# The border between two trunk layers: squares summed in two groups of eight, and the first weight splits of layer 1 in an order fixed by hand

## The chip, the cores and the metric

The kernel runs on one core of a Trainium2 chip. A core has five engines that run side by side and meet through semaphores: TensorE (PE in the profile, with its weight loads as PEld), VectorE (DVE), ScalarE (ACT), GpSimd (POOL) and SyncE (SP, which here only issues DMAs). Each engine works through its own instructions in order. The metric is the device time of one execution in microseconds (us), as the median of several runs. In this kernel a difference of about 0.2% can be told from no change.

## The reference, cut to what matters

Two layers work on 256 latent tokens and 256 context tokens of width 2048. In each layer both streams are normalised, scaled and shifted, go through one wide input projection, three mixing branches and an output projection. The border is the end of layer 0 and the start of layer 1 for the latents:

```
for l in range(DEPTH):
    ...
    h = rmsnorm(x, g_pre[l]) * (1.0 + scale[:, None]) + shift[:, None]
    proj = h @ w_in[l]
    ...
    y = rmsnorm(y @ w_out[l], g_post[l])
    x_new = x + gate[:, None] * y
```

So at the border the output projection y of layer 0 is divided by its own root mean square and added to x, which gives x1; then the root mean square of x1 over all 2048 features must be known before the first h of layer 1 exists. Everything is float32.

## The kernel before, in words

**Layout.** Activations lie transposed: `yo[k]`, k = 0 to 15, holds 128 features by 512 tokens, the latents in columns 0 to 255 (`LAT`), the context in the rest (`CTX`). `hh[k]` and `hl[k]` are the input of a projection, split into a high part (a cast to a shorter float32 form) and a low part (the difference), so that a product takes three matmuls (`mm3`, L424 to L426).

**Weights.** `Stream` brings the weights in tiles of 128 x 1024. SP loads a tile into `raw` (L382, three buffers, shared with the tiles of x that the border reads, L1118). ACT casts it to `whi` (L402), DVE subtracts to get `wlo` (L404); four buffers each. I call the first three tiles of layer 1 w0, w1 and w2. The first block of layer 1 (k = 0 and 1, `start_av` and `start_au`) needs w0 and w1, the second block w2.

**Who sets the order.** PE's instructions run in the order in which the program writes them. DVE, ACT and SP are ordered by a planner that models times and priorities; `low(n)` lowers a priority, and `tc.issue_after(x)` puts an instruction behind x on x's engine, without a semaphore. `W.behind` lists, for a weight tile by its number, what its cast must stand behind.

**The held units.** The last three output units of layer 0 (`HELD = 3`) are computed for the latents first and for the context afterwards (`hold_unit`). The context part is 48 steps of three matmuls, and covers the border's chain on PE. After each step `later.tick` adds 0.324 to a counted clock (0.648 x 256 / 512), and a task whose time has come writes its next piece into PE's order at that place. So a task's `yield` value sets after which of the 48 steps its next matmuls stand.

**The border** is the task `boundary`:

- `rms_of`: sums of y's squares (`col_sums`, L462), mean on DVE (L452), the power -1/2 on POOL (L454), spread over 128 partitions by PE (`bcast`, L475).
- For each k: DVE multiplies `yo[k]` by the factor (L1128), DVE (even k) or POOL (odd k) adds x (L1129), ACT squares it (L1132).
- PE sums the squares over the partitions with `ones`, four k side by side in four column strips (L1139). Before, this stands in four groups of four squares, after steps 15, 19, 23 and 27.
- DVE copies the sums to SBUF (`row`, L1143); PE adds the four strips (L1147, after step 30); DVE and POOL make the factor (L452, L454); PE spreads it (L475, after step 38); DVE copies it (L1152). After step 48 layer 1 begins.
- `make_h` for k = 0 and 1: DVE (L502), ACT (L506, the high part), DVE (L511, the low part).

The context part of the last three units is scaled and squared by `o_evac` (ACT L996 and L520, DVE L521) at a low priority.

Before, the casts of w0 and w1 stand behind the high part of h for k = 1 (`W.behind = {len(W.out): made, len(W.out) + 1: made}`).

Of the kernel before, what the change touches and what calls it, by code (L numbers as in the profile page):

```python
# [7 lines left out]
F32 = mybir.dt.float32  # L8
F32R = mybir.dt.float32r
BF16 = mybir.dt.bfloat16  # L10
AF = mybir.ActivationFunctionType
ALU = mybir.AluOpType

P = 128
D = 2048
KT = D // P
S = 256
T = 2 * S
EPS = 1e-6
# [47 lines left out]
def trunk_kernel(ctx: ExitStack, tc: tile.TileContext, xT, xhalf, cT, wss, wsl, wmod, win, wout0, wout1, const, vec, rows,  # L67
                 wmat, bs, sink, out):
    nc = tc.nc
    V, A, G, PE, DMA = nc.vector, nc.scalar, nc.gpsimd, nc.tensor, nc.sync  # L70
# [6 lines left out]
    def sb(shape, dt, tag, bufs=1):  # L77
        cnt[0] += 1
        return pool.tile(shape, dt, tag=tag, bufs=bufs, name=f"{tag}_{cnt[0]}")

    def w2k(shape, dt=F32):
        return sb(shape, dt, "w2k", W2K)

    def mm_ps(name="mm"):
        cnt[0] += 1
        return psum.tile([P, 512], F32, tag="mm", bufs=6, name=f"ps_{name}_{cnt[0]}")
# [6 lines left out]
    yo = [sb([P, T], F32, f"yo{k}") for k in range(KT)]  # L93
# [13 lines left out]
    class low:  # L107


        def __init__(self, n):  # L110
            self.n = n
# [8 lines left out]
    def cc(name):  # L120
        o, w = COFF[name]
        return cst[:, o - P:o - P + w]
# [151 lines left out]
    state = {"ctx": [], "phase": "", "owed": 0.0}  # L274
# [14 lines left out]
    GATES = {2: 0, 14: 1}, {7: 2}, {12: 3}, {}  # L289
    YG = 3.0  # L290
    YH = 2.0
    NX, LATE = 4, 12
    YX, YR, YC, YE = 1.0, 0.8, 1.5, 5.0
    YX1 = 12.0
    YQ, YA, YB = [5.5, 6.0], [10.0, 8.0], [3.8, 4.0]

# [45 lines left out]
    class Stream:  # L342
        AHEAD = 3

        def __init__(self):
            self.src, self.out, self.pos, self.stop = [], [], 0, 0
            self.raws = []
            self.place, self.behind = {}, {}
            for l in range(2):
                def half(name, i, h):  # L350
                    return win[l, UIDX[name][i], h]
                for i in range(2):
                    a = [half("av", 2 * i, 0), half("au01", i, 0), half("av", 2 * i, 1),
                         half("av", 2 * i + 1, 0), half("au01", i, 1), half("av", 2 * i + 1, 1)]
                    if l == 0:
                        a.insert(3 - i, half("au2", 0, i))
                        self.place[len(self.src) + 3 - i] = AU2[i]
                    self.src += a
                for i, u in enumerate(UNITS):
                    if u[0] not in ("av", "au01") + ("au2",) * (l == 0):  # L360
                        self.src += [win[l, i, 0], win[l, i, 1]]
                if l == 0:
                    self.src += [wout0[j, i] for j in range(KT) for i in range(2)]
                else:
                    self.src += [wout1[c, i] for c in range(4) for i in range(8)]
                if l == 0:
                    n = len(self.src) - 2 * HELD
                    self.place[n] = (("mraw", 2), ("mraw", 2))
                    self.place[n + 1] = (("macc", 1), ("mg", 1))
            for i, tags in enumerate(TAIL):  # L370
                self.place[len(self.src) - len(TAIL) + i] = tags
            self.raw_place = {len(self.src) - len(TAILRAW) + i: tags for i, tags in enumerate(TAILRAW)}
# [12 lines left out]
        def emitting(self, cut=1024):  # L385

            if len(self.raws) == len(self.out):
                self.load()
            n = len(self.out)
            r = self.raws[n]  # L390
            tags = self.place.get(n, (("whi", NHI), ("wlo", NLO)))
            hi, lo = ([sb([P, 1024 // len(t[0].split())], F32R, tag, t[1]) for tag in t[0].split()] for t in tags)
            self.out.append((hi, lo))
            cut = min(cut, 1024 // max(len(hi), len(lo), len(r) if isinstance(r, list) else 1))
            for i in range(0, 1024, cut):
                c = slice(i, i + cut)
                ph, pl = part((hi, lo), c)
                rc, _ = part((r, r), c)
                with ExitStack() as after:
                    for i in self.behind.get(n, ()):  # L400
                        after.enter_context(tc.issue_after(i.ins))
                    A.copy(ph, rc)  # L402
                yield
                self.last = V.tensor_tensor(out=pl, in0=rc, in1=ph.bitcast(F32), op=ALU.subtract)  # L404
                yield

        def emit(self):
# [13 lines left out]
    W = Stream()  # L421
# [6 lines left out]
    def part(w, c):  # L428

        def of(t):  # L430
            if not isinstance(t, list):
                return t[:, c]
            n = t[0].shape[-1]
            return t[c.start // n][:, c.start % n:c.start % n + c.stop - c.start]

        return of(w[0]), of(w[1])
# [12 lines left out]

    def rstd_cols(sums, n, dim):  # L450
        t = sb([P, 4], F32, "rs_a", 2)
        V.tensor_scalar(out=t[:, :n], in0=sums, scalar1=1.0 / dim, scalar2=EPS, op0=ALU.mult, op1=ALU.add)  # L452
        r = sb([P, 4], F32, "rs_b", 2)
        state["pow"] = G.tensor_tensor(out=r[:, :n], in0=t[:, :n], in1=mhalf[:, :n], op=ALU.pow)  # L454
        return r
# [67 lines left out]
    FULL, LAT, CTX = slice(0, T), slice(0, S), slice(S, T)  # L523
# [48 lines left out]
    def layer(l):  # L572
        last = l == 1
        n = S if last else T
# [16 lines left out]
        def take(k, which=(0,)):  # L591

            for i in which:
                if k % (2, 4, 8)[i] == 0:
                    ws_[i] = W.next()

        def start_av(k, ts):
            avw = ws_[0]
            c = slice((k % 2) * 512, (k % 2 + 1) * 512)
            for t in ts:  # L600
                sl = slice(t * P, (t + 1) * P)
                mm3(av[t], h_of(l, k, sl), part(avw, c), k == 0, k == KT - 1)
# [13 lines left out]
        if l == 0:  # L616
            made = {}
# [86 lines left out]
        for i, (k0, nk) in enumerate(blocks if l else ()):  # L704
            for k in range(k0, k0 + nk):
                made = make_h(1, k, rbs[0], [0])
            if i == 0:
                W.behind = {len(W.out): made, len(W.out) + 1: made}
                with tc.issue_after(made[0].ins), tc.issue_after(made[1].ins):
                    state["late"]()  # L710
            take(k0, (0, 1))
            start_av(k0, range(nt))
            if nk == 2:
                start_au(k0)
                start_av(k0 + 1, range(nt))
            start_au(k0 + nk - 1)
            if k0 == 8:
                border()
# [385 lines left out]
    def rms_of(s, acc, wait):  # L1104

        ps = ms_ps("rs")
        col_sums(ps, acc, 2)
        r = rstd_cols(ps[:, 0:2], 2, D)
        yield wait
        return bcast(r, 2)[:, 0:S]  # L1110

    def boundary(acc):

        x0s = []

        def load():
            x0s.append(sb([P, 4, S], F32, "raw", NRAW))
            DMA.dma_start(x0s[-1], xhalf[0, len(x0s) - 1])  # L1118

        for _ in range(2):  # L1120
            load()
        r0 = yield from rms_of(0, acc[:, LAT], 2.2)
        cs_ps = mm_ps("rs2")
        pend = []
        for k in range(KT):
            if k in (4, 8):
                load()
            V.tensor_tensor(out=yo[k][:, LAT], in0=yo[k][:, LAT], in1=r0, op=ALU.mult)  # L1128
            (G if k % 2 else V).tensor_tensor(out=yo[k][:, LAT], in0=yo[k][:, LAT], in1=x0s[k // 4][:, k % 4],  # L1129
                                              op=ALU.add)  # L1130
            q = w2k([P, S])
            A.activation(q, yo[k][:, LAT], AF.Square)  # L1132
            pend.append(q)
            if k % NX == NX - 1:
                yield YX
                for i, q in enumerate(pend):
                    kk = k + 1 - len(pend) + i
                    c = slice(32 * (kk % 4), 32 * (kk % 4) + 32)
                    PE.matmul(cs_ps[c, 0:S], ones[:, 0:32], q, start=kk < 4, stop=kk >= KT - 4,  # L1139
                              tile_position=(0, 32 * (kk % 4)))  # L1140
                pend = []
        row = w2k([P, S])
        V.tensor_copy(row, cs_ps[:, 0:S])  # L1143
        yield YR
        ps = ms_ps("rs")
        for j in range(2):
            PE.matmul(ps[:, j:j + 1], row[:, j * P:(j + 1) * P], cc("sel")[:, 0:1], start=True, stop=True)  # L1147
        r = rstd_cols(ps[:, 0:2], 2, D)
        yield 2.4
        rb = bcast(r, 2)  # L1150
        r = sb([P, S], F32, "rbs", 2)
        V.tensor_copy(r, rb[:, 0:S])  # L1152
        rbs[0] = r
# [46 lines left out]
    def border():  # L1200
        later.add(lowered(boundary_ctx(state["acc"])))
# [3 lines left out]
    with tc.manual_schedule(engines={EN.PE}):  # L1205
# [12 lines left out]
        for k in range(KT):  # L1218
            q = w2k([P, T])
# [7 lines left out]
        row = w2k([P, T])  # L1227
# [106 lines left out]
```

## Time and profile before

| | us |
|---|---|
| median of 3 runs (1141.18 to 1142.53) | 1141.69 |
| the profiled execution | 1141.21 |
| its span, first to last instruction | 1139.4 |
| PE busy | 1126.1 |
| DVE busy | 879.9 |
| ACT busy | 515.4 |
| POOL busy | 31.7 |

The mean granted TensorE clock is 0.998 of full speed, and DMAs move 206 GB/s on average. Between 726.5 and 746.0 us of the span, the border, PE is busy for 19.30 of 19.50 us, DVE for 12.31, ACT for 10.21 and POOL for 7.48.

In a timeline a row gives the start in us from the span's start, the duration in us, the engine, the line, the operation, the tiles (out<-in) and how many instructions are merged; in brackets stands how long the engine was idle before it and what released it. Ends of matmuls are modelled, so for PE the starts are what to read.

### The profile page before, as it was taken

The page shows a single profiled execution, that of the slowest core. Times are in us where ns is not written, and L with a number is a line of the kernel's source. Part 1 is how long each engine was busy: PE and PEld are TensorE (multiplying, and loading weights), DVE is VectorE, ACT ScalarE, POOL GpSimd, SP SyncE. Part 2 cuts the span into 40 slices and gives each one's busy share as a digit, 9 for nine tenths or more (in the row PEclk, how much of TensorE's full clock was granted, in tenths as well). Part 3 has the DMA queues.
Part 4 walks back from the last instruction along what each step waited for, and adds up shares of the span by engine and source line. Part 5 has one row for each costly group of instructions (what it writes and reads, how often), then busy time and mean ns, then how long its engine had stood idle before and what let it go on. Part 6 is the DMA issues. An engine that isn't in the chain of part 4 may idle for free.

```text
span 1139.4 us, 16858 instructions
## 1 busy us (share of the span) xinstructions
PE 1126.1 (99%) x6335; PEld 932.0 (82%) x6339; DVE 879.9 (77%) x1480; ACT 515.4 (45%) x933; POOL 31.7 (3%) x39
## 2 busy tenths in 40 slices
PE   8999999999999999999999999999999999999997
PEld 3567788888898888888888888887898988888885
DVE  1545498999987787888999993397788689868884
ACT  5222422322335667632532333365655369856551
POOL 0000000000000000000000000205000000000001
PEclk9999999999999999999999999999999999999999
DMA  9999665556655343355466664258756675555872
GB/s 353 394 390 402 243 198 194 182 185 217 201 176 175 112 139 128 106 200 184 152 220 212 215 189 143 74 177 210 221 179 211 217 274 194 170 159 194 298 260 74
DMA packets 72658, 234.28 MB, mean 206 GB/s; under 512 B 8448, under 2 KB 11392, under 8 KB 72576
## 3 DMA queue, kind: packets, MB, share of 16 engines
q1 hardware_dynamic: 70272, 231.11, 60.0%
q0 software_dynamic: 2304, 2.10, 1.2%
q8 instruction: 49, 0.80, 0.3%
q14 instruction: 33, 0.27, 0.1%
HBM read 231.08 MB, written 2.10 MB: 205 GB/s over the span
## 4 chain that ended last, share of the span: by engine, by line
PE 96%; DMA 2%; DVE 1%; ACT 0%; SPq 0%; issue 0%; POOL 0%; DVEq 0%; POOLq 0%; ACTq 0%
PE ps_t L424 14%; PE ps_t L426 14%; PE ps_t L425 14%; PE ps_t L540 10%; PE ps_t L541 5%; PE ps_y L424 3%; PE ps_y L426 3%; PE ps_y L425 3%; PE ps_mod L169 2%; PE ps_av L424 2%; PE ps_cx L426 2%; PE ps_cx L424 2%; PE ps_cx L425 2%; PE ps_av L425 2%; PE ps_av L426 2%; PE ps_tp L910 2%
## 5 line engine op out<-in xcount | busy, mean ns | idle before, releaser
L402 ACT CAST whi<-raw 128x1024 fp32r<-128x1024 f32 (+1 forms) x216 | 224.1, 1041 | 327.6 <-PE ps_t L425 193.4
L404 DVE TENSOR_TENSOR wlo<-raw,whi 128x1024 fp32r<-128x1024 f32 (+1 forms) x216 | 260.3, 1209 | 67.4 <-ACT whi L402 65.8
L424 PE MATMUL ps_t<-hh,whi 128*128 128x512 f32 (+1 forms) x704 | 268.2, 381 | 0.0
L426 PE MATMUL ps_t<-hh,wlo 128*128 128x512 f32 (+1 forms) x704 | 267.6, 380 | 0.0
L425 PE MATMUL ps_t<-hl,whi 128*128 128x512 f32 (+1 forms) x704 | 267.4, 380 | 0.0
L207 DVE SCALAR_TENSOR_TENSOR macc<-mraw,cs,macc 128x512 f32<-128x512 f32 x360 | 248.7, 744 | 15.1 <-DMA mraw<-in_wmod_dram 14.5
L540 PE MATMUL ps_t<-hh,whi 128*128 128x512 f32 x448 | 163.7, 402 | 0.0
L426 PEld LDWEIGHTS ps_t<-hh,wlo 128*128 128x128 f32 x704 | 132.4, 188 | 25.2
L424 PEld LDWEIGHTS ps_t<-hh,whi 128*128 128x128 f32 x704 | 132.4, 188 | 25.0 <-issue 1.2
L425 PEld LDWEIGHTS ps_t<-hl,whi 128*128 128x128 f32 x704 | 132.4, 188 | 23.7
L541 PE MATMUL ps_t<-hh,wlo 128*128 128x256 f32 x448 | 125.7, 281 | 0.0
L540 PEld LDWEIGHTS ps_t<-hh,whi 128*128 128x128 f32 x448 | 84.2, 188 | 19.1 <-issue 0.5
L541 PEld LDWEIGHTS ps_t<-hh,wlo 128*128 128x128 f32 x448 | 84.7, 189 | 0.5 <-issue 0.5
L506 ACT ACTIVATE hh<-w2k,sh 128x256 fp32r<-128x256 f32 x48 | 21.8, 502 | 78.5 <-DVE w2k L502 78.5
L424 PE MATMUL ps_y<-whi,hh 128*128 128x512 f32 x104 | 41.3, 397 | 0.0
L426 PE MATMUL ps_y<-whi,hh 128*128 128x512 f32 x104 | 40.6, 390 | 0.0
L425 PE MATMUL ps_y<-wlo,hh 128*128 128x512 f32 x104 | 40.5, 389 | 0.0
L424 PE MATMUL ps_av<-whi,hh 128*128 128x512 f32 x96 | 39.9, 415 | 0.6 <-ACT hh L506 0.6
L424 PE MATMUL ps_cx<-whi,hh 128*128 128x512 f32 x96 | 38.7, 403 | 0.0
L425 PE MATMUL ps_av<-wlo,hh 128*128 128x512 f32 x96 | 38.0, 396 | 0.4 <-DVE wlo L404 0.4
L425 PE MATMUL ps_cx<-wlo,hh 128*128 128x512 f32 x96 | 37.3, 389 | 0.0
L441 ACT CAST w2k<-ps_tp 128x512 fp32r<-128x512 f32 x40 | 23.4, 584 | 23.1 <-PE ps_scc L425 12.7
(398 smaller groups left out, 1860.4 us busy)
## 6 DMA issues: line engine op xcount, KB each, us to landing
raw<-in_win_dram SPq DMA_DIRECT2D x160, 512.0 KB, 4.1
mraw<-in_wmod_dram SPq DMA_DIRECT2D x128, 512.0 KB, 4.3
raw<-in_wout_dram SPq DMA_DIRECT2D x60, 512.0 KB, 4.3
mraw<-in_wsl_dram SPq DMA_DIRECT2D x16, 512.0 KB, 6.6
yo<-in_xT_dram SPq DMA_DIRECT2D x16, 256.0 KB, 5.2
macc<-in_wsl_dram SPq DMA_DIRECT2D x8, 512.0 KB, 7.6
vv<-in_wsl_dram SPq DMA_DIRECT2D x8, 512.0 KB, 8.1
mg<-in_wsl_dram SPq DMA_DIRECT2D x8, 512.0 KB, 8.0
```

What stands on the lines that cost most here:

```text
L169: PE.matmul(ps[32 * kk:32 * kk + 32, 0:n], cpad[:, kg * 4 + kk], ws[kk], start=kg == 0, stop=kg == 3, tile_position=(0, 32 * kk))
L207: V.scalar_tensor_tensor(out=acc[:, s], in0=w[:, kk % 2], scalar=c, in1=acc[:, s], op0=ALU.mult, op1=ALU.add)
L402: A.copy(ph, rc)
L404: self.last = V.tensor_tensor(out=pl, in0=rc, in1=ph.bitcast(F32), op=ALU.subtract)
L424: PE.matmul(ps, st[0], mv[0], start=start, stop=False)
L425: PE.matmul(ps, st[0], mv[1], start=False, stop=False)
L426: PE.matmul(ps, st[1], mv[0], start=False, stop=stop)
L441: A.copy(hi, src)
L506: first = A.activation(h_of(l, k, sl)[0], t[:, sl], AF.Identity, bias=sh[l][:, k, s:s + 1])
L540: PE.matmul(ps, w[0], h, start=k == 0, stop=False)
L541: PE.matmul(ps[:, 0:S], w[1], h[:, 0:S], start=False, stop=k == KT - 1)
L910: PE.transpose(tp[:, (2 * j + b) * P:(2 * j + b + 1) * P], src, ident)
```

## The change

Four things change in the code, all at the border.

1. The squares are summed in two groups of eight. ACT writes them in pairs into one buffer. `YX` holds two waits, 4.9 and 2.2 units, in place of four of 1.0.
2. The waits after the sums are shorter: 0.5 units in place of 0.8 before the strips are added, 1.2 in place of 2.4 before the factor is spread.
3. The casts of w0 and w1 on ACT stand behind the last square, and the cast of w2 behind the high part of h for k = 1.
4. The subtractions on DVE get a place of their own (`W.under`): w0's behind the copy of the sums (L1143), w1's behind the mean (L452), w2's behind the low part of h for k = 1.

```
-    NX, LATE = 4, 12
-    YX, YR, YC, YE = 1.0, 0.8, 1.5, 5.0
+    LATE = 12
+    YX, YR, YB1 = [4.9, 2.2], 0.5, 1.2
+    YC, YE = 1.5, 5.0
...
-                self.last = V.tensor_tensor(out=pl, in0=rc, in1=ph.bitcast(F32), op=ALU.subtract)
+                with ExitStack() as after:
+                    if n in self.under:
+                        after.enter_context(tc.issue_after(self.under[n].ins))
+                    self.last = V.tensor_tensor(out=pl, in0=rc, in1=ph.bitcast(F32), op=ALU.subtract)
...
-        V.tensor_scalar(out=t[:, :n], in0=sums, scalar1=1.0 / dim, scalar2=EPS, op0=ALU.mult, op1=ALU.add)
+        state["sum"] = V.tensor_scalar(out=t[:, :n], in0=sums, scalar1=1.0 / dim, scalar2=EPS, op0=ALU.mult,
+                                       op1=ALU.add)
...
-                W.behind = {len(W.out): made, len(W.out) + 1: made}
+                w0 = len(W.out)
+                W.behind = {w0: state["last"], w0 + 1: state["last"], w0 + 2: made}
+                W.under = {w0: state["row"], w0 + 1: state["mean"], w0 + 2: made[1]}
...
-            q = w2k([P, S])
-            A.activation(q, yo[k][:, LAT], AF.Square)
+            if k % 2 == 0:
+                pair = w2k([P, 2, S])
+            q = pair[:, k % 2]
+            square = A.activation(q, yo[k][:, LAT], AF.Square)
             pend.append(q)
-            if k % NX == NX - 1:
-                yield YX
+            if k % 8 == 7:
+                yield YX[k // 8]
...
-        V.tensor_copy(row, cs_ps[:, 0:S])
+        state["last"], state["row"] = [square], V.tensor_copy(row, cs_ps[:, 0:S])
         yield YR
...
-        yield 2.4
+        state["mean"] = state["sum"]
+        yield YB1
```

More of the change, by code (lines that the diff above doesn't have):

```diff
@@ L347, in __init__ @@
             self.raws = []
-            self.place, self.behind = {}, {}
+            self.place, self.behind, self.under = {}, {}, {}
             for l in range(2):
```

## The prediction

> **What bounds the kernel now.** I read the page first, then the list of what PE waited for, then the timelines of the border engine by engine.
>
> ```profile
> span 1139.4 us, 16858 instructions
> PE 1126.1 (99%) x6335; PEld 932.0 (82%) x6339; DVE 879.9 (77%) x1480; ACT 515.4 (45%) x933; POOL 31.7 (3%) x39
> PE 96%; DMA 2%; DVE 1%; ACT 0%; SPq 0%; issue 0%; POOL 0%; DVEq 0%; POOLq 0%; ACTq 0%
> ...
> PE ps_mix L761 <- DVE mgl L442: 1.1, 1, 1.1
> ...
> PE ps_av L425 <- DVE wlo L404: 0.4, 1, 0.4
> ```
>
> The first three lines are of the page. PE is busy for 99% of the span and is 96% of the chain that ended last. So the time is what PE has to do and the few places where it stands. The last two lines are of PE's waits: after the border's sums only two are left, 0.4 us for the first `wlo` of layer 1 and 1.1 us at a mix of layer 1. From the border to the end nothing else holds PE, so a microsecond taken off PE's line at the border should arrive at the end. Now PE's starts at the border:
>
> ```profile
> 726.15 0.60 PE L475 MATMUL ps_rb<-identr,rs_b 128*128 128x128 f32 x4
> ...
> 727.90 0.28 PE L426 MATMUL ps_t<-hh,mg 128*128 128x256 f32 x1
> ...
> 730.51 0.38 PE L424 MATMUL ps_t<-hh,macc 128*128 128x256 f32 x1
> ...
> 734.27 0.28 PE L426 MATMUL ps_t<-hh,wlo 128*128 128x256 f32 x1
> ...
> 735.05 0.38 PE L424 MATMUL ps_t<-hh,whi 128*128 128x256 f32 x1
> ...
> 736.67 0.64 PE L1139 MATMUL ps_rs<-w2k,ones 128*32 128x256 f32 x8
> ...
> 738.42 0.50 PE L1147 MATMUL ps_rs<-cst,w2k 128*128 128x1 f32 x4
> ...
> 741.74 0.60 PE L475 MATMUL ps_rb<-identr,rs_b 128*128 128x128 f32 x4
> 742.10 0.36 PE L424 MATMUL ps_t<-hh,whi 128*128 128x256 f32 x1
> 742.30 0.28 PE L425 MATMUL ps_t<-hl,whi 128*128 128x256 f32 x1
> ...
> 745.77 0.39 PE L424 MATMUL ps_av<-whi,hh 128*128 128x512 f32 x1
> ...
> 750.62 0.40 PE L424 MATMUL ps_av<-whi,hh 128*128 128x512 f32 x1
> ...
> 754.80 0.40 PE L424 MATMUL ps_av<-whi,hh 128*128 128x512 f32 x1
> ```
>
> - One held matmul: from 742.30 to 745.77 there are 29, so 0.1197 us each.
> - A small insertion (the factor, or the strips): 742.10 - 741.74 = 0.36, and the first matmul behind it takes 0.20 in place of 0.12. Together 0.44.
> - A group of four squares: from 734.27 to 735.05 are 0.78, less the 0.12 that the matmul takes, plus 0.10 behind it: 0.76. The first group takes 2.61 - 0.12 + 0.10 = 2.59, because its squares weren't there: 1.8 us of standing that the list of waits hides inside busy matmuls.
> - From the first factor at 726.15 to layer 1 at 745.77 are 19.62: 37 steps of three (13.29), three insertions (1.32) and four groups (5.01, so the second and fourth take some 1.7 together).
> - The first block of layer 1 takes 750.62 - 745.77 = 4.85, the second 4.18: the wait for w0's `wlo` costs 0.67.
>
> **The groups.** With the new `yield` values the task's places, counted in steps of 0.324, are: first group after step 27 (16 steps behind the factor at step 11), second after 34, strips after 36, factor after 40, with 8 steps left. How long eight squares take is seen in layer 0, where four strips of the same shape are summed four deep:
>
> ```profile
> 51.19 0.39 PE L425 MATMUL ps_av<-wlo,hh 128*128 128x512 f32 x1
> 51.41 0.39 PE L426 MATMUL ps_av<-whi,hl 128*128 128x512 f32 x1
> ...
> 53.59 0.50 PE L424 MATMUL ps_av<-whi,hh 128*128 128x512 f32 x1
> ```
>
> 53.59 - 51.41 less a step of 0.22 is 1.96 for four deep. One deep is 0.66 (the 0.76 without what lies behind it), so a further depth costs (1.96 - 0.66)/3 = 0.43, and a group of eight 0.76 + 0.43 = 1.19. PE's line becomes 13.29 + 1.32 + 2 x 1.19 = 16.99 in place of 19.62: 2.63 less, if nothing is late.
>
> **Are the squares there?**
>
> ```profile
> 731.54 0.71 ACT L1132 ACTIVATE w2k<-yo 128x256 f32<-128x256 f32 x2
> ...
> 735.83 0.42 ACT L1132 ACTIVATE w2k<-yo 128x256 f32<-128x256 f32 x1 [0.27 <-POOL yo L1129]
> ...
> 744.23 1.98 ACT L402 CAST whi<-raw 128x1024 fp32r<-128x1024 f32 x2
> ```
>
> The squares of k = 6 and 7 end at 732.25. PE reaches the first group at 726.15 + 0.44 + 48 x 0.1197 + 0.09 = 732.43 (0.09 being the switch into a group) and its second half 0.43 later. The last square ends at 736.25; PE is at the second group at 732.34 + 1.19 + 21 x 0.1197 + 0.09 = 736.13, and at its second half at 736.56. So I cost the squares at nothing, under covers of 0.6 and 0.3 us. If ACT takes an `o_evac` of a held unit ahead of the last square, some 0.8 us, PE stands 0.5.
>
> Writing in pairs takes eight buffers of the seven that the tag has, so the seventh pair waits for the first group. That has begun at 732.43, and the seventh pair's first square (k = 12) comes well behind the 732.25 at which k = 7 ends, at 0.5 us each: some 2.4 later. Nothing.
>
> **The casts of w0 and w1.** They move to 736.25, right behind the last square, and take 1.98 together, in a time where ACT idles. What is queued behind them is the evacuation of a held unit, which nobody waits for soon. w1's tile must have landed (the second row is of the view of the tile `raw` from 700 to 760 us):
>
> ```profile
> 733.53 0.33 SPq L382 DMA_DIRECT2D raw<-in_win_dram  x1
> ...
> DMA to landing us min/median/max: 3.3/3.8/4.8
> ```
>
> The DMA of w1 is issued at 733.53, when the border's third tile of x comes free, and that doesn't move. It lands at 737.3 by the median (736.8 to 738.3), so its cast ends at about 738.3. No DMA of w0 to w2 is issued otherwise than before; w3's comes earlier, since w0's buffer comes free earlier.
>
> **The subtractions, and what they stand in front of.**
>
> ```profile
> 737.46 0.42 DVE L1143 COPY w2k<-ps_rs 128x256 f32<-128x256 f32 x1 [2.27 <-PE ps_rs L1139]
> 738.96 0.16 DVE L452 TENSOR_SCALAR rs_a<-ps_rs 128x2 f32<-128x2 f32 x1 [1.07 <-PE ps_rs L1147]
> 742.38 0.42 DVE L1152 COPY rbs<-ps_rb 128x256 f32<-128x256 f32 x1 [1.39 <-PE ps_rb L475]
> ...
> 743.96 0.88 DVE L511 SCALAR_TENSOR_TENSOR hh<-w2k,sh,hh 128x256 fp32r<-128x256 f32 x2 [0.24 <-ACT hh L506]
> 745.29 2.36 DVE L404 TENSOR_TENSOR wlo<-raw,whi 128x1024 fp32r<-128x1024 f32 x2 [0.45 <-ACT whi L402]
> ```
>
> The copy of the sums starts 0.79 behind a group's start (737.46 - 736.67), and 0.43 later for eight: 736.13 + 1.22 = 737.35. w0's subtraction follows 0.32 later, at 737.67, and holds DVE for 1.13 (two in a row take 2.36, one 1.23), until 738.80. PE adds the strips at 726.15 + 0.44 + 75 x 0.1197 + 2 x 1.19 = 737.95, and L452 could run 0.54 later (738.96 - 738.42), at 738.49. So the mean comes 0.31 late, at 738.80.
>
> w1's subtraction stands directly behind the mean, so it runs beside POOL's power, which the border's chain waits for. In the border before, DVE was idle there. Later in the trace the same three instructions do stand together:
>
> ```profile
> 739.26 0.71 POOL L454 TENSOR_TENSOR rs_b<-rs_a,mhalf 128x2 f32<-128x2 f32 x1 [3.47 <-DVE rs_a L452]
> ...
> 828.81 0.16 DVE L452 TENSOR_SCALAR rs_a<-ps_rs 128x2 f32<-128x2 f32 x1 [0.20 <-PE ps_rs L462]
> 828.89 1.23 DVE L404 TENSOR_TENSOR wlo<-raw,whi 128x1024 fp32r<-128x1024 f32 x1
> ...
> 829.12 1.57 POOL L454 TENSOR_TENSOR rs_b<-rs_a,mhalf 128x2 f32<-128x2 f32 x1 [34.11 <-DVE rs_a L452]
> ...
> 734.78 0.41 DVE L521 TENSOR_TENSOR acc<-acc,w2k 128x256 f32<-128x256 f32 x1
> ...
> 734.60 1.19 POOL L1129 TENSOR_TENSOR yo<-yo,raw 128x256 f32<-128x256 f32 x1
> ```
>
> The power takes 0.71 beside an idle DVE and 1.57 beside a subtraction that began 0.23 earlier; it ends 0.57 after the subtraction. POOL's add at 734.60 likewise ends 0.60 after DVE's L521. So between 0.71 and 1.57 I take 1.57, the row with the same two neighbours.
>
> The Trainium skill says the same of it, and more strictly (SBUF — State Buffer, "Who interferes with whom"): a VectorE instruction with two SBUF inputs and a GpSimd instruction that reads SBUF exclude each other, and the second one waits for the whole of the first. By that rule alone, with the full 0.71 behind the subtraction's end, the power would end 0.14 later than by the row, which makes 1139.5 of the sum; this hangs on w1's subtraction starting first.
>
> So the power starts 0.30 behind the mean (739.26 - 738.96), at 739.10, and ends at 740.67 (739.81 without the neighbour). PE is at the factor's place at 737.95 + 0.44 + 12 x 0.1197 = 739.83. It stands from there to about 740.72, and loses 0.10 more in starting again. Layer 1 begins at 740.72 + 0.44 + 24 x 0.1197 + 0.10 = 744.13.
>
> **Is h there?** The copy L1152 stands 0.64 behind the factor's start (742.38 - 741.74), and both low parts are done 2.46 after the copy's start (743.96 + 0.88 - 742.38): 743.82 against 744.13. w0 and w1 are ready since about 740.0, so the 0.67 of the first block goes. w2's cast ends at about 744.3 and its subtraction at 745.5; the second block begins at 744.13 + 4.18 = 748.3. DVE has 2.26 us of subtractions less to do from there, so nothing is late next; the cover is 2.8 us.
>
> **The sum.** 745.77 + 0.67 - 744.13 = 2.31 us less. On the profiled execution (span 1139.4, time 1141.21) that is a span of 1137.1; the median of the runs lies 0.48 above that execution, so I count from the median: 1141.69 - 2.31 = 1139.4.
>
> **Rivals.**
>
> - *The power isn't held up.* If w1's tile lands later than 737.9, or the planner puts its subtraction elsewhere, the power ends at 739.81, PE hardly stands, and layer 1 begins at 743.17: 3.3 us less, 1138.4. For it: the landing may take up to 4.8. Against it: the median leaves 0.6 us.
> - *The power is held longer.* If w0's cast is late, both subtractions run behind the mean (738.57 to 740.83); the power ends 0.58 later, layer 1 begins at 744.87: 1.6 less, 1140.1. An L521 behind w1's subtraction would give 1139.7. For it: the add at 734.60 was held by such an L521. Against it: w0's cast ends at 737.2, 0.4 before it is needed.
> - *Given back in layer 1.* The planner orders DVE and ACT anew from here on, and one place is near the limit: ACT waits for a context tile ahead of what the mix needs.
>
> ```profile
> 781.10 0.42 ACT L1175 ACTIVATE acc<-yo 128x256 f32<-128x256 f32 x1 [3.73 <-DMA yo<-in_xhalf_dram]
> ```
>
>   If that DMA doesn't come earlier with the rest, ACT stays at 781.10, the mix (1.1 us of waiting already) stays where it is, and the gain is gone: 1141.7. Against it: the DMA hangs on a factor that PE makes at a counted step, so it should shift too.
> - *Slower.* The same place on the other side: with DVE's work ordered otherwise, two subtractions (2.26) ahead of the multiplication that feeds that DMA, it lands at 783.4, and PE waits that much more at the mix: 1144.0. It decides from 2.3 us behind today's 781.10. Nothing in the profile points there except that the place waits already.
>
> **How the numbers follow.** Chances: as summed 0.42 (1139.0 to 1139.8), power free 0.20, power held longer 0.16, given back 0.10, slower 0.12. 0.2%, or 2.3 us, is about what a measurement of this kernel can tell from no change, and my sum lies right at that bound, so I split the likeliest case: faster 0.20 + 0.24 = 0.44, same 0.18 + 0.16 + 0.10 = 0.44, slower 0.12. The range from 1138.2 to 1141.9 leaves out the slower case and the edge of the power-free one.
>
> **What would show it.** Two groups of 16 on L1139, each some 1.2 us of PE's line; casts of w0 and w1 at about 736.3 and 737.3; w0's subtraction ahead of L452; L454 at about 739.1 with 1.57 and not 0.71; PE waiting for POOL at L475 by 0.9; no wait at the first `wlo`; layer 1 beginning at 744.1. The prediction is wrong if the squares hold either group, if the power is free, or if the wait at the mix grows.

## The result, and the profile after

The changed kernel takes 1137.90 us in the median of six runs (1137.23 to 1138.82), the kernel before 1142.11 us beside it (six runs, 1140.96 to 1143.65). The ratio is 0.9969, with a 95% interval from 0.9959 to 0.9978. Measured again later, in eleven runs, it gave 1138.65 us and a ratio of 0.9980 (0.9971 to 0.9990). The forecast was 1139.4 us, or 0.9980 of 1141.69: 2.3 us less, where the two comparisons have 4.21 and 3.07 less. The profiled execution took 1138.35 us, 2.86 less than the one before.

The head and the chain of the page after:

```profile
span 1136.6 us, 16851 instructions
PE 1123.4 (99%) x6335; PEld 931.8 (82%) x6339; DVE 879.8 (77%) x1480; ACT 514.4 (45%) x933; POOL 32.5 (3%) x39
PE 96%; DMA 2%; DVE 0%; SPq 0%; issue 0%; ACT 0%; POOL 0%; DVEq 0%; POOLq 0%
```

PE is still the bound. Its busy time fell by 2.7 us with the same 6335 instructions. Most of that is a matmul's waiting inside its group, which counts as busy: the first group of squares of before is 2.20 us busy, and the fourth, of the same size, 0.64 (736.67 in the prediction).

```profile
728.38 2.20 PE L1139 MATMUL ps_rs<-w2k,ones 128*32 128x256 f32 x8 [0.20 <-ACT w2k L1132]
```

PE's timeline after, in the order of the rows quoted of before:

```profile
726.16 0.60 PE L480 MATMUL ps_rb<-identr,rs_b 128*128 128x128 f32 x4
...
732.44 1.07 PE L1148 MATMUL ps_rs<-w2k,ones 128*32 128x256 f32 x16
...
736.14 1.16 PE L1148 MATMUL ps_rs<-w2k,ones 128*32 128x256 f32 x16
...
738.05 0.50 PE L1156 MATMUL ps_rs<-cst,w2k 128*128 128x1 f32 x4
...
739.93 0.66 PE L480 MATMUL ps_rb<-identr,rs_b 128*128 128x128 f32 x4
...
743.29 0.40 PE L428 MATMUL ps_av<-whi,hh 128*128 128x512 f32 x1
...
747.47 0.40 PE L428 MATMUL ps_av<-whi,hh 128*128 128x512 f32 x1
...
788.66 0.71 PE L768 MATMUL ps_mix<-ws,w2k 128*128 128x128 f32 x4 [1.30 <-DVE mgl L446]
```

The first factor comes at 726.16 (726.15 before), layer 1 at 743.29 (745.77): 2.48 less. The first block takes 747.47 - 743.29 = 4.18 in place of 4.85, so the wait of 0.67 is gone. But PE waits 1.30 at the mix, where it waited 1.07. And PE stands nowhere for the factor, which the forecast had at 744.13 - 743.17 = 0.96 of layer 1's start. DVE, ACT, POOL and SP of the same execution show why:

```profile
733.54 0.33 SPq L383 DMA_DIRECT2D raw<-in_win_dram  x1
...
737.35 0.42 DVE L1152 COPY w2k<-ps_rs 128x256 f32<-128x256 f32 x1 [2.13 <-PE ps_rs L1148]
737.69 1.22 DVE L408 TENSOR_TENSOR wlo<-raw,whi 128x1024 fp32r<-128x1024 f32 x1
738.82 0.15 DVE L456 TENSOR_SCALAR rs_a<-ps_rs 128x2 f32<-128x2 f32 x1
739.29 1.22 DVE L408 TENSOR_TENSOR wlo<-raw,whi 128x1024 fp32r<-128x1024 f32 x1 [0.31 <-ACT whi L403]
...
738.21 1.05 ACT L403 CAST whi<-raw 128x1024 fp32r<-128x1024 f32 x1 [0.65 <-DMA raw<-in_win_dram]
...
739.12 0.71 POOL L459 TENSOR_TENSOR rs_b<-rs_a,mhalf 128x2 f32<-128x2 f32 x1 [3.31 <-DVE rs_a L456]
```

w1's tile landed at 738.21, 4.67 after its issue. ACT waited 0.65 for it, so w1's subtraction began 0.17 behind the power, and the power took 0.71.

The second group of squares took 1.09 us up to the next held matmul (736.14 to 737.23), the first 1.00 (732.44 to 733.44). ACT had taken an evacuation of a held unit (L1003) ahead of the last two squares:

```profile
735.53 0.47 ACT L1003 ACTIVATE yo<-ps_t,gg 128x256 f32<-128x256 f32 x1 [0.30 <-PE ps_t L430]
735.91 0.72 ACT L1141 ACTIVATE w2k<-yo 128x256 f32<-128x256 f32 x2
```

The last square ends at 736.63, and the matmuls that read it begin at 736.68, so it held the group by some 0.09.

### The profile page after: what moved, and what is told of

The parts are those of the page before. It is cut to its first block, busy times and chain, and to the rows that moved or that the text cites. A ratio compares the mean times of both kernels' runs of the same rounds, so it can differ in the third digit from the quotient of the medians.

```text
span 1136.6 us, 16851 instructions
## 1 busy us (share of the span) xinstructions
PE 1123.4 (99%) x6335; PEld 931.8 (82%) x6339; DVE 879.8 (77%) x1480; ACT 514.4 (45%) x933; POOL 32.5 (3%) x39
## 4 chain that ended last, share of the span: by engine, by line
PE 96%; DMA 2%; DVE 0%; SPq 0%; issue 0%; ACT 0%; POOL 0%; DVEq 0%; POOLq 0%
PE ps_t L428 14%; PE ps_t L429 14%; PE ps_t L430 14%; PE ps_t L545 10%; PE ps_t L546 5%; PE ps_y L428 3%; PE ps_y L430 3%; PE ps_y L429 3%; PE ps_mod L169 2%; PE ps_av L428 2%; PE ps_cx L430 2%; PE ps_cx L428 2%; PE ps_cx L429 2%; PE ps_av L429 2%; PE ps_av L430 2%; PE ps_tp L917 2%
## 5 line engine op out<-in xcount | busy, mean ns | idle before, releaser
L207 DVE SCALAR_TENSOR_TENSOR macc<-mraw,cs,macc 128x512 f32<-128x512 f32 x360 | 249.2, 746 | 17.8 <-DMA mraw<-in_wmod_dram 17.4
```

Source lines behind the costliest of these rows:

```text
L207: V.scalar_tensor_tensor(out=acc[:, s], in0=w[:, kk % 2], scalar=c, in1=acc[:, s], op0=ALU.mult, op1=ALU.add)
```

## The experiments

All are edits of the changed kernel, but for "before, mix later". For each, the profile is laid on one ruler: PE's starts counted from its first factor of the border, which comes between 725.7 and 727.3 us by execution. "Last" is the last output matmul of layer 1. Power: its duration, and by how much w1's subtraction began ahead of it.

| | ratio to before (95%) | layer 1 begins | second block | last | power (ahead) | wait at the mix |
|---|---|---|---|---|---|---|
| before | | 19.62 | 24.47 | 404.77 | 0.71 (-) | 1.07 |
| changed | 0.9969 (0.9959 to 0.9978) | 17.13 | 21.31 | 401.90 | 0.71 (-0.17) | 1.30 |
| changed, again | 0.9980 (0.9971 to 0.9990) | 17.98 | 22.15 | 401.67 | 1.55 (0.23) | 0.29 |
| groups only | 0.9984 (0.9975 to 0.9992) | 17.35 | 22.62 | 402.54 | 0.71 (-) | 0.60 |
| weights only | 0.9993 (0.9985 to 1.0002) | 19.63 | 23.80 | 403.26 | 0.71 (-1.48) | 0.25 |
| no places for the subtractions | 0.9989 (0.9980 to 0.9998) | 18.55 | 22.72 | 402.72 | 0.75 (-) | 0.55 |
| strips later | 0.9986 (0.9977 to 0.9995) | 18.49 | 22.66 | 402.51 | 1.57 (0.23) | 0.64 |
| old waits | 0.9983 (0.9975 to 0.9992) | 17.80 | 22.14 | 401.46 | 1.57 (0.23) | 0 |
| four late groups | 0.9985 (0.9976 to 0.9994) | 18.65 | 22.82 | 402.15 | 1.55 (0.23) | 0 |
| mix later | 0.9968 (0.9955 to 0.9980) | 18.14 | 22.31 | 401.25 | 1.72 (0.07) | 0 |
| mix and factor later | 0.9964 (0.9951 to 0.9977) | 17.30 | 21.47 | 400.67 | 1.60 (0.19) | 0 |
| before, mix later | 0.9987 (0.9978 to 0.9996) | 19.63 | | 403.56 | | 0 |

### The groups alone

The casts and subtractions go back behind the high part of h; the shorter waits behind the sums stay.

```
-                W.behind = {w0: state["last"], w0 + 1: state["last"], w0 + 2: made}
-                W.under = {w0: state["row"], w0 + 1: state["mean"], w0 + 2: made[1]}
+                W.behind = {w0: made, w0 + 1: made}
+                W.under = {}
```

> The two groups of eight and the shorter waits alone; the casts of w0 and w1 stand behind the high part of h again, and the subtractions have no place of their own. Theory (the gain is the sum of two parts, 2.6 us of PE's line from the groups and the rest from the weights being ready): layer 1 still begins at about 743.3, but its first products then wait for w0's low part, which comes about 1.9 us behind both low parts of h, at 744.9, so PE stands some 1.4 us there; the time is 1.5 to 1.8 us below the kernel before (ratio 0.9985). Rival (the groups bring it all): no wait at the first low part, 3 us less. Rival (the weights bring it all): no change.

PE's timeline of this run at the start of layer 1:

```profile
744.19 0.49 PE L428 MATMUL ps_av<-whi,hh 128*128 128x512 f32 x1
745.45 0.50 PE L429 MATMUL ps_av<-wlo,hh 128*128 128x512 f32 x1 [0.77 <-DVE wlo L408]
```

The second block comes 24.47 - 22.62 = 1.85 sooner than before. With no subtraction near the power, PE's line runs through to the end of the held units: its last held step lies 17.08 from the factor with the matmul that follows counted in (743.80 + 0.12 - 726.84), against the 16.99 of the forecast for "if nothing is late"; the last square holds the second group here too (1.09 against 1.00). Then layer 1 stands 0.27 for w0's high part, whose cast now ends after PE is there, and 1.09 in its first block (749.46 - 744.19 - 4.18). That block stood 0.67 before: PE came sooner, the weights did not.

### The weights alone

Groups of four at the old places, with the new order of casts and subtractions.

```
-    YX, YR, YB1 = [4.9, 2.2], 0.5, 1.2
+    YX, YR, YB1 = [1.0, 1.0, 1.0, 1.0], 0.8, 2.4
...
-            if k % 8 == 7:
-                yield YX[k // 8]
+            if k % 4 == 3:
+                yield YX[k // 4]
```

The pairs become single buffers again.

> The order of the weights' splits alone; four groups of four squares with the waits of before. Theory (sum of two parts): PE's line at the border keeps its 19.62 us, with the 1.8 us in the first group; layer 1 begins at 745.8, and only the 0.67 us at the first low part goes: ratio 0.9994, within what can be told from no change. Rival (the weights bring it all): 3 us less, 0.9972.

Layer 1 begins where it did (19.63), and the second block 0.67 sooner: the wait for `wlo`, and nothing else. The interval of the ratio reaches over 1. The parts add up to 1.85 + 0.67 = 2.52 of the 3.16 that both together take off the way to the second block. The 0.64 that is missing is what the groups alone give back in layer 1: 1.09 - 0.67 in the first block, and 0.22 ahead of it (17.35 - 17.13).

### No places for the subtractions

```
-                W.under = {w0: state["row"], w0 + 1: state["mean"], w0 + 2: made[1]}
+                W.under = {}
```

> The changed kernel without the places of the subtractions on VectorE; the planner then puts the subtractions of w0 and w1 ahead of the copy of the sums and ahead of the mean. Theory (the order by hand is worth what it keeps out of the chain): w0's subtraction runs at 737.6 to 738.8, the copy of the sums at 738.8 and not 737.35, w1's subtraction waits for its late cast (739.3) in front of the mean, the mean comes at 740.5 and not 738.8; PE stands some 1.2 us ahead of the strips and 0.4 us ahead of the factor; layer 1 begins at about 744.9, 1.6 us later than with the order by hand. Rival (the order on VectorE is indifferent, PE has cover): layer 1 begins at 743.3 and the time is the changed kernel's.

DVE's and PE's timelines of this run:

```profile
738.72 1.23 DVE L408 TENSOR_TENSOR wlo<-raw,whi 128x1024 fp32r<-128x1024 f32 x1 [2.37 <-ACT whi L403]
739.86 0.42 DVE L1152 COPY w2k<-ps_rs 128x256 f32<-128x256 f32 x1
740.20 1.22 DVE L408 TENSOR_TENSOR wlo<-raw,whi 128x1024 fp32r<-128x1024 f32 x1
741.33 0.15 DVE L456 TENSOR_SCALAR rs_a<-ps_rs 128x2 f32<-128x2 f32 x1
```
```profile
740.33 0.61 PE L1156 MATMUL ps_rs<-cst,w2k 128*128 128x1 f32 x4 [0.99 <-DVE w2k L1152]
```

The planner puts w0's subtraction ahead of the copy of the sums and w1's ahead of the mean. PE stands 0.99 at the strips, and layer 1 begins 1.42 later than in the first profile of the changed kernel. Without the places on DVE, the casts' going forward brings nothing over the groups alone: the second block begins at 22.72 here, at 22.62 there.

### Is the power's price an accident of the landing? The changed kernel again

Nothing is edited.

> The changed kernel once more, nothing edited. The theory that the landing of w1's tile decides the price of POOL's power: if w1's subtraction begins before the power, the power takes 1.5 to 1.7 us and layer 1 begins 17.9 to 18.1 us after the first factor; if it begins after the power, the power takes 0.71 us and layer 1 begins 17.1 us after it. The rival, that the order of the instructions alone decides: 0.71 us and 17.13 us again, whatever the landing. The time by both about 0.9969 of the kernel before.

The same rows of this execution:

```profile
738.57 1.22 DVE L408 TENSOR_TENSOR wlo<-raw,whi 128x1024 fp32r<-128x1024 f32 x1
...
738.80 1.55 POOL L459 TENSOR_TENSOR rs_b<-rs_a,mhalf 128x2 f32<-128x2 f32 x1 [3.31 <-DVE rs_a L456]
...
740.41 0.71 PE L480 MATMUL ps_rb<-identr,rs_b 128*128 128x128 f32 x4 [0.65 <-POOL rs_b L459]
...
743.83 0.40 PE L428 MATMUL ps_av<-whi,hh 128*128 128x512 f32 x1
...
788.19 0.71 PE L768 MATMUL ps_mix<-ws,w2k 128*128 128x128 f32 x4 [0.29 <-DVE mgl L446]
```

Here ACT cast both tiles in a row, w1's subtraction began 0.23 ahead of the power, and the power took 1.55. Layer 1 begins 743.83 - 725.85 = 17.98 behind the factor, which is the forecast's 744.13 - 726.15 to the last digit. One program, two prices: the written order does not decide which of the two starts first, the landing of w1's tile does. Yet the whole is not longer: 401.67 to the last output matmul against 401.90, as the mix waits 0.29 and not 1.30. The expected ratio of 0.9969 lies just outside this comparison's interval (0.9971 to 0.9990).

### The strips later

```
-    YX, YR, YB1 = [4.9, 2.2], 0.5, 1.2
+    YX, YR, YB1 = [4.9, 2.2], 1.2, 0.5
```

> The strips are added two steps later (after step 38 in place of 36), the factor's place stays after step 40; so the mean comes at about 739.3, when w1's cast has just ended, and w1's subtraction starts directly behind the mean and ahead of POOL's power. Theory of the prediction (the second of the two waits for the first): the power takes 1.5 to 1.6 us and not 0.71, ends at about 741.2, PE stands 1.3 us ahead of the factor, and layer 1 begins at about 744.6: 1.3 us above the changed kernel, 1.6 to 2 below the one before. Rival (they don't disturb each other): the power takes 0.71, PE stands 0.4 us, layer 1 begins at 743.8.

The strips move from step 36 to 38, the factor stays after step 40. The mean comes at 13.15 from the factor in place of 12.65 (the run just told), the power takes 1.57, and PE stands 1.15 for it in place of 0.65:

```profile
740.74 0.71 PE L480 MATMUL ps_rb<-identr,rs_b 128*128 128x128 f32 x4 [1.15 <-POOL rs_b L459]
```

So 0.50 later at the mean is 0.50 later at the factor. With the power held, the chain from the mean to the factor has no slack. The power takes what the theory said, and not the rival's 0.71.

### The old waits behind the sums

```
-    YX, YR, YB1 = [4.9, 2.2], 0.5, 1.2
+    YX, YR, YB1 = [4.9, 2.2], 0.8, 2.4
```

> The changed kernel with the old waits behind the sums: strips after step 37, factor after step 45 in place of 36 and 40. Theory (the last three steps of held products don't cover the making of h): the factor starts at about 741.7 and not 739.9, both parts of h for k = 0 are ready at 744.4, PE is at layer 1 at 743.25 and stands 0.6 to 0.9 us in the first block; ratio to the kernel before 0.9976. Rival (h comes in time anyway): no wait in the first block, the changed kernel's ratio.

The factor stands five steps later. The power is held here too (1.57), but PE doesn't wait for it. It waits for h instead (PE's waits from 724 to 800 us):

```profile
PE ps_av L428 <- ACT hh L511: 0.6, 1, 0.6
PE ps_av L430 <- DVE hh L516: 0.2, 1, 0.2
```

The second block begins at 22.14, as in the second run of the changed kernel (22.15). So the shorter waits of the change gain nothing when the power is held. Against the execution with a free power they gain 0.83 (22.14 - 21.31); PE doesn't wait for the power with the old waits, so a free one should not help them, but no profile shows that.

### Four groups, but late

The groups of four, in single buffers as with the weights alone, stand after steps 21, 26, 30 and 34, where their squares are there; the rest is as changed.

```
-    YX, YR, YB1 = [4.9, 2.2], 0.5, 1.2
+    YX, YR, YB1 = [3.0, 1.5, 1.2, 1.2], 0.5, 1.2
```

> The changed kernel with four groups of four squares again, but after steps 21, 26, 30 and 34, where the squares are there; everything behind the last group as in the changed kernel. Theory (of the 2.5 us by which PE's line got shorter, 1.8 are the wait in the first group and 0.66 the two groups less): from the first factor to layer 1 PE needs 17.13 + 0.66 = 17.8 us, 1.8 us less than with four groups at the old places; 0.66 us above the changed kernel, ratio to the kernel before 0.9975. Rival (the number of groups is what counts): 19 us and more, ratio 0.9985 or above.

The power is held again and PE stands 0.74 for it, so the run is compared with the held run of the changed kernel: 18.65 - 17.98 = 0.67 later, of which 0.09 is more standing. The forecast's sizes, 0.76 for a group of four and 1.19 for one of eight, make 4 x 0.76 - 2 x 1.19 = 0.66 for the number of groups. So of the 2.63 that the two groups save, some 0.6 to 0.7 comes of there being two, and the rest of their squares being there. The theory's 17.8 and 0.9975 were worked out with a free power; the ratio came out at 0.9985, where the rival has it, though its 19 us did not come.

### The wait at the mix

The mix's first step moves by 1.4 units, so PE does other matmuls first.

```
-            yield 11.0 if l == 0 else 7.0
+            yield 11.0 if l == 0 else 8.4
```

> The changed kernel with one number altered: the first mix of layer 1's spatial gating stands 1.4 units later in PE's order (the first yield of branch_a is 8.4 in place of 7.0 for layer 1), some 1.5 us of PE's time. In the changed kernel PE stands 1.30 us there for a PSUM bank that VectorE frees behind two weight subtractions. Theory (that wait is on PE's line and nothing else stands behind it): the wait goes, 1.3 us less than the changed kernel, ratio to the kernel before 0.9957. Rival (the wait moves to a later mix, or the planner's new order makes another): the changed kernel's ratio, 0.9969.

No wait at the mix is left. In this execution the power is held (1.72) and PE stands 0.82 for it, which the first profile of the changed kernel didn't; the ratio, 0.9968, is no better than the first one of the changed kernel, and the expected 0.9957 did not come. From the factor to the last output matmul it is 0.42 shorter than the held run (401.25, 401.67).

Where the wait comes from shows when the profiles are laid side by side. Ahead of the mix, ACT squares the first context tile (L1185, L1175 before), and that waits for a DMA of POOL's queue that adds x into the tile (L1168, L1158 before). POOL's issues, of which the row's start is the first, and ACT's square, of before (its square is the row at 781.10 in the prediction), of the changed kernel, of its second run and of this one:

```profile
775.79 7.40 POOL L1158 DMA_DIRECT2D yo<-in_xhalf_dram  x8 [4.97 <-DVE yo L1166]
```
```profile
772.64 7.37 POOL L1168 DMA_DIRECT2D yo<-in_xhalf_dram  x8 [5.85 <-DVE yo L1176]
778.16 0.42 ACT L1185 ACTIVATE acc<-yo 128x256 f32<-128x256 f32 x1 [3.94 <-DMA yo<-in_xhalf_dram]
```
```profile
773.17 7.38 POOL L1168 DMA_DIRECT2D yo<-in_xhalf_dram  x8 [5.85 <-DVE yo L1176]
777.68 0.42 ACT L1185 ACTIVATE acc<-yo 128x256 f32<-128x256 f32 x1 [2.94 <-DMA yo<-in_xhalf_dram]
```
```profile
773.36 7.40 POOL L1168 DMA_DIRECT2D yo<-in_xhalf_dram  x8 [5.85 <-DVE yo L1176]
778.62 0.42 ACT L1185 ACTIVATE acc<-yo 128x256 f32<-128x256 f32 x1 [3.67 <-DMA yo<-in_xhalf_dram]
```

| | issue to square | square to mix | wait at the mix |
|---|---|---|---|
| before | 5.31 | 10.50 | 1.07 |
| changed | 5.52 | 10.50 | 1.30 |
| changed, again | 4.51 | 10.51 | 0.29 |
| groups only | 4.82 | 10.51 | 0.60 |
| weights only | 4.53 | 10.50 | 0.25 |
| strips later | 4.90 | 10.51 | 0.64 |
| no places | 4.81 | 10.51 | 0.55 |
| old waits | 3.78 | 10.83 | 0 |
| four late groups | 4.34 | 10.51 | 0 |
| mix later | 5.26 | 10.70 | 0 |
| mix and factor later | 4.42 | 11.53 | 0 |

The issue follows PE: it lies 29.35 behind layer 1's start in the changed kernel (772.64 - 743.29), 29.34 in its second run, and 30.02 before, where the first block stood 0.67. But the transfer takes 3.8 to 5.5 us by execution. The mix can begin 10.5 us after the square, and PE waits what the transfer takes over about 4.2 us (the 0.1 of the four late groups is too little to be listed). With the mix later, a transfer of 5.26 costs no wait. POOL's issuing is not what differs: the first of the eight issues takes 1.05 or 1.06 in every profile. Nor is it the chip alone: the three runs old waits, four late groups and mix later were on one chip, with 3.78, 4.34 and 5.26.

The same edit alone on the kernel before:

> The kernel before, with only the next mix's steps later (8.4 units in place of 7.0). The theory that PE's wait at the mix is set by the landing of the first context tile's accumulating DMA (the mix can begin 10.5 us after the square that waits for it) and that the landing differs by execution: PE comes to the mix some 1.35 us later in its own line, so no wait there in any landing up to 5.5 us; from the first factor to the last output matmul of ps_y 403.7 us in place of 404.77; the time 0.9990 to 0.9995 of the kernel before, and the runs lie within about 1 us of each other where those of the kernel before lie within 3. The rival, that the wait comes of the order of the instructions and only moves with it: a wait of about 1 us stays at the mix or behind it, the ratio is 1.000, and the runs spread as before.

Its transfer took 5.15 (775.96 to 781.11), and PE's waits from 724 to 800 us are those of the border alone:

```profile
PE ps_av L425 <- DVE wlo L404: 0.4, 1, 0.4
PE ps_rs L1139 <- ACT w2k L1132: 0.2, 1, 0.2
```

From the first factor to the last output matmul it is 403.56, 1.21 less than before, and the ratio is 0.9987 (0.9978 to 0.9996). That speaks for the landing and against the order. The expected narrower spread did not come: eleven runs lie between 1139.45 and 1142.29, so in the kernel before the transfer is not what spreads the runs. The five runs each of the two changed kernels with the mix later lie within 0.6 and 0.8; that is too few to tell.

### The two together

```
-    YX, YR, YB1 = [4.9, 2.2], 0.5, 1.2
+    YX, YR, YB1 = [4.9, 2.2], 0.5, 1.8
...
-            yield 11.0 if l == 0 else 7.0
+            yield 11.0 if l == 0 else 8.4
```

> The next mix's steps later (as in the run in which only these are later) and the factor two blocks later than in the changed kernel, after step 42. The theory: with the power held up by w1's subtraction TensorE stands about 0.25 us at the factor's copies in place of 0.82, so layer 1 begins about 17.5 us after the first factor (17.1 if the power is not held up); no wait for a bank of the mix; the first context product 65.3 to 65.5 us after the first factor (66.97 in the changed kernel, 65.97 with the mix's steps later alone); the time 0.9960 of the kernel before. The rival: h comes late to the first block, TensorE stands there instead, and the time is 0.9968 as with the mix's steps later alone.

The factor stands two steps later (after step 42). POOL's and PE's timelines:

```profile
738.94 1.60 POOL L459 TENSOR_TENSOR rs_b<-rs_a,mhalf 128x2 f32<-128x2 f32 x1 [3.31 <-DVE rs_a L456]
...
740.59 0.71 PE L480 MATMUL ps_rb<-identr,rs_b 128*128 128x128 f32 x4
743.29 0.40 PE L428 MATMUL ps_av<-whi,hh 128*128 128x512 f32 x1
```

The power is held until 740.54, and PE begins the factor at 740.59; h is in time. PE still stands some 0.2 there, as expected: the matmul before it began at 740.34, 0.25 earlier in place of 0.12, and the next one begins 0.47 later (741.06) in place of 0.36. Layer 1 begins at 17.30, where 17.5 was expected. From the border up to 800 us the list of PE's waits is empty; it leaves out waits as short as that. The first context product at 65.36 answers to the expected 65.3 to 65.5, but not for that reason alone: with the mix later, the mix's second step stands behind that product and not ahead of it, so this mark flatters both runs. By the last output matmul it is 400.67, against 401.67 and 401.90 of the changed kernel. The five runs take 1136.94 to 1137.74, median 1137.10; ten of the eleven runs of the changed kernel on this chip took longer than the slowest of them. Its ratio is the lowest here, though the interval overlaps those of the changed kernel and of the mix later alone.

## Why the prediction was right, and where it failed

- **The sign and the size.** Faster, at 0.9969 and 0.9980 where the sum gave 0.9980. The time was forecast 1.5 us too high beside the first comparison and 0.75 beside the second. The prediction gave "faster" and "same" a chance of 0.44 each, so it left open whether the gain would stand clear of the noise. The profiles show 2.87 and 3.10 less up to the last output matmul; what the first comparison has beyond that (4.21) no profile accounts for. In the first profile all three of the prediction's own signs of being wrong are there: squares that hold a group, a free power, a longer wait at the mix. That the time lies in the range all the same is owed to the terms that held, the groups and the first block.
- **The groups.** Forecast at 732.43 and 736.13, measured at 732.44 and 736.14. From one group's start to the next are 3.70, which holds 1.19 for a group. Right but for one thing: "I cost the squares at nothing" failed by 0.09. ACT took half of an evacuation ahead of the last squares, as the prediction had feared, and the last one ended at 736.63 and not at 736.25, past its cover of 0.3.
- **The copy, w0's subtraction, the mean.** Forecast at 737.35, 737.67 and 738.80; measured at 737.35, 737.69 and 738.82. The factor's place was forecast at 739.83 and is 739.93, as the strips came 0.10 later than summed, by that square. Right.
- **The power: the step that failed.** "Between 0.71 and 1.57 I take 1.57" rested on w1's tile landing after the median of 3.8 us. It took 4.67, the subtraction came second, and the power took 0.71. The median was that of all tiles of the stretch; in the eight profiles in which w1's cast moves forward and waits for nothing but its tile, the tile took 4.06 (there at most) to 4.67, so the cover of 0.6 was never there. The rival "the power isn't held up" came true there: layer 1 at 743.17 by that rival, 743.29 measured. In the second execution the tile was in time, and the step held: 1.55 and 17.98. The power was held in five more profiles (strips later, old waits, four late groups, mix later, both later); with the weights alone w1's subtraction began 1.48 behind the power and left it free, because ACT's cast of w1 stood 2.48 there, by the profile for PE and not for the tile. With the strips after step 36, a tile after 4.06, 4.30 and 4.42 put the subtraction 0.23, 0.19 and 0.07 ahead of the power, and one after 4.67 put it 0.17 behind: by these four the border lies at some 4.5 (an estimate). So the row was the likelier one, but both prices belong to the same program; I should have carried the landing's spread (3.3 to 4.8, which I had quoted) through to the power's price.
- **w0 and w1 at the first block.** The 0.67 goes, as summed, and the weights alone show just that. What the sum didn't say is that this wait would have grown to 1.09 had only the groups moved.
- **The mix.** "The wait at the mix grows" stood among the signs of a wrong prediction, and it grew, 1.07 to 1.30. I had found the place (the square that waits for a context tile's DMA) and argued that the transfer would shift with the factor. Its issue does; its duration doesn't repeat. I took 1.07 as a fixed term, where profiles without the later mix show 0 to 1.30.
- **A slip in a rival.** In "the power is held longer" the end of both subtractions, 740.83, and the 0.57 behind it make 741.40, 0.73 and not 0.58 later than 740.67; its 744.87 and 1140.1 go with the 0.73.
- **The account.** Of the first profile, 404.77 - 401.90 = 2.87 less: 2.49 at the border and 0.67 at the first block, less 0.23 at the mix, leaves 2.93. Of the second, 3.10 less: 1.64 + 0.67 + 0.78 = 3.09. What the first gained more at the border it gave back at the mix; that the two end alike is chance.

Open: what makes w1's tile land between 4.06 and 4.67 after its issue, and the context tile's transfer take 3.8 to 5.5. I had no run on that.

## What to carry to other kernels

When a step's price depends on which of two instructions starts first, look at what each of them waits for: if one waits for a DMA, the price is a spread and not a number, and one profile shows one draw of it. A wait at the end of a chain that hangs on a DMA is such a draw too; move the waiting engine's own work in front of it by the width of the spread, and it need cost nothing: with the mix later, none of three profiles has the wait. Bringing one thing earlier is worth its whole time only if what the next stage needs comes earlier with it: the groups alone lost 0.64 us of their gain to weights that were not there.

## What the runs showed of the hardware

DVE and POOL held each other up here, each way round. With DVE's subtraction of two SBUF tiles first by 0.07 to 0.23 us, POOL's power takes 1.55 to 1.72 and ends about 0.57 behind the subtraction. With the power first by 0.17, the power takes its usual 0.71 and the subtraction its usual 1.22: nobody waits. That one profile does not make the exclusion one-sided. At the very end of the same execution DVE is the one that waits:

```profile
1124.68 1.84 DVE L1085 SCALAR_TENSOR_TENSOR yo<-yo,rs_b,mg 128x512 f32<-128x512 f32 x1
1124.68 1.29 POOL L1083 TENSOR_TENSOR yo<-yo,kt 128x512 f32<-128x512 f32 x1 [0.83 <-ACT yo L1082]
1126.44 0.74 DVE L1085 SCALAR_TENSOR_TENSOR yo<-yo,rs_b,mgl 128x512 f32<-128x512 f32 x1
```

Both engines read two SBUF tiles, and the two records begin together. DVE's instruction takes 1.84, where the next one, of the same shape and with no neighbour, takes 0.74, and it ends 0.55 behind POOL's. This comes twice in each of the twelve profiles, with 1.81 to 1.85. The Trainium skill (SBUF — State Buffer, "Who interferes with whom") has whichever of the two comes second wait for the whole of the first. The rows agree, where DVE's subtraction is first and where the two begin together, that one waits for the other to end, though the power's tail is 0.57 and not the 0.71 of a power by itself. Where the 128x2 power is first (739.12 and 739.29 in the first profile) no waiting of DVE shows, and there the measurement decides; for what part of its 0.71 the power would hold DVE off, no run here shows.

The other thing is the size of the differences between transfers that are alike: issued at the same place of the same program, the first context tile's transfer took 5.52 us in one execution and 4.51 in another.
